# The first pair of K tiles: halved loads on two hardware queues, and copies divided over two engines

## The chip, the cores and the metric

The kernel runs on one core of one Trainium2 chip. The metric is the time of one execution on the device, in microseconds, as the median of several runs. The core has a matrix engine (TensorE, PE in the profile), a vector engine (VectorE, DVE), a scalar engine (ScalarE, ACT), a general engine (GpSimd, POOL) and a queue engine (SyncE, SP). Transfers are issued by SP, ACT and POOL, each into a queue of its own, and 16 DMA engines serve all of these queues.

## The reference

The inputs are float32: `a` and `b` are 2048 x 2048, `gamma` has 2048 elements, `eps` is 1e-5.

```python
x = np.matmul(a, b)
rms = np.sqrt(np.mean(x ** 2, axis=-1, keepdims=True) + eps)
return (gamma * x / rms).astype(np.float32)
```

Every row of the product is divided by its root mean square and multiplied by `gamma`.

## The kernel before, in words

Rows of `a` are handled in 16 blocks of 128. K is cut into 16 tiles of 128, which are taken in eight *pairs*. B has a left and a right half of 1024 columns, and each half has two chunks of 512. TensorE needs A with K on the partitions, so A is transposed first.

The work has three stages. In the *head*, row blocks 0 to 3 are multiplied by the left half of B while both arrive, pair by pair. Then the same four blocks meet the right half, and after that the other twelve blocks follow in groups of two, by seven products in place of eight (Strassen's scheme, with sums of quarters made on VectorE). In the last stage each block is scaled and stored.

The change touches the head alone, and in it pair 0. For pairs 1 to 7 of the head, POOL issues two loads each (`load_head`, L104): 128 columns by two of A for four row blocks into `early`, and the two tiles of B's left half into `raw` (L99). Both convert float32 to bfloat16 on the way. They are issued in the order of the pairs, pairs 1 to 3 at the start (L128, L131), pair 4 and later from within the loop over the pairs (L436). POOL's ninth and later loads each wait for the landing of the one issued eight before, since a completion semaphore is used again; this keeps eight loads in flight.

Pair 0 goes another way. Its part of A (`a0f`, 512 rows of 256 columns) is loaded as float32 by SP, and its two tiles of B (`b0f[0]` and `b0f[1]`, 128 x 1024 each) as float32 by ACT. Both lie in `early`. In `transpose_first` (L150) TensorE transposes A's eight 128 x 128 blocks, four of K tile 0 into one PSUM bank and four of K tile 1 into another. Each bank is moved to `head_at`, as bfloat16, in two moves of 128 x 256. Each tile of B is cast to bfloat16 in two halves of 512 columns, the first by VectorE and the second by ScalarE, into `raw[0][0]`. All four moves are on VectorE. Ahead of this, TensorE does eleven matmuls of zeros (L145), which nothing reads.

After it, `stream` (L397) does the pair's matmuls: seven (row block, chunk) groups for K tile 0, then the same seven for K tile 1. The order of the groups is (block 0, chunk 0), (block 0, chunk 1), (block 1, chunk 0) and so on, so the second matmul reads the second half of the cast tile. After twelve matmuls of pair 0 (seven in later pairs) TensorE transposes A of the next pair (`transpose_head`, L167), and VectorE copies that bank to `head_at` (L177). The eighth group, block 3 with chunk 1, has no accumulator of its own for the whole head; its two matmuls of a pair go to the bank that the transposes use (`stream_in_parts`, L411, L415), so they wait for VectorE's copy at L177.

The order on every engine is the order in which the program is written: the schedule is manual. Semaphores for the data are added by the framework.

Of the kernel before, what the change touches and what calls it, by code (L numbers as in the profile page):

```python
# [17 lines left out]
def kernel(  # L18
# [13 lines left out]
    nc = tc.nc  # L32
    P = 128
# [4 lines left out]
    W2 = 2 * P  # L38
    MB = M // P
    CH = 512  # L40
    NCH = N // CH
    HALF = N // 2
    HB = 4
# [16 lines left out]
    head_at = consts.tile([P, KT, HB, P], BF16, name="head_at")  # L60
    raw = [[consts.tile([P, 2, HALF], BF16, name=f"b_{j}_{kp}") for kp in range(KP)]
           for j in range(2)]
# [4 lines left out]
    a0f = early[:, 0:2048].bitcast(FP32).rearrange("p (r k) -> p r k", r=HB)  # L67
    b0f = [early[:, 2048 + t * 2048:2048 + (t + 1) * 2048].bitcast(FP32) for t in range(2)]
# [19 lines left out]
        return (at_even, at_odd)[(mb // 2) % 2][:, mb % 2]  # L88


    nc.sync.dma_start(out=a0f, in_=a[0:HB * P, 0:W2].rearrange("(r p) k -> p r k", p=P))
    for t in range(2):
        nc.scalar.dma_start(out=b0f[t], in_=b[t * P:(t + 1) * P, 0:HALF])

    def ah(kp):
        return ah_slot[(kp - 1) % NAH]
# [53 lines left out]
    def transpose_first():  # L150
        bank = [ps_t.tile([P, CH], FP32, name="tbank"), ps_a.tile([P, CH], FP32, name="acc")]
        view = [b.rearrange("p (r m) -> p r m", r=HB) for b in bank]
        for t in range(2):
            for r in range(HB):
                nc.tensor.matmul(view[t][:, r, :], a0f[:, r, t * P:(t + 1) * P], identity_f,
                                 is_transpose=True, start=(r == 0), stop=(r == HB - 1))
        for t in range(2):
            cast_first = [lambda: nc.vector.tensor_copy(out=raw[0][0][:, t, :CH],
                                                        in_=b0f[t][:, :CH]),
                          lambda: nc.scalar.copy(out=raw[0][0][:, t, CH:], in_=b0f[t][:, CH:])]  # L160
            move = [lambda h=h: nc.vector.tensor_copy(
                out=head_at[:, t, 2 * h:2 * h + 2, :], in_=view[t][:, 2 * h:2 * h + 2, :])
                for h in range(2)]
            for work in (cast_first + move if t == 0 else move + cast_first):
                work()

    def transpose_head(kp):  # L167
        bank = ps_t.tile([P, CH], FP32, name="tbank")
# [263 lines left out]
    for r in range(HB):  # L432
        x_tile(r, 0)
    early_sums = {4: ((2,), 0, 6), 5: ((5,), 0, 7), 6: ((1,), 0, KP)}
    transpose_first()
    for kp in range(KP):  # L436
        if kp + 4 < KP:
# [391 lines left out]
```

## Time and profile before

| What | us |
|---|---|
| median of 7 runs | 222.59 (222.46 to 222.88) |
| profiled execution | 222.4 |
| its span on the core | 220.6 |
| TensorE busy | 209.0 (95% of the span) |
| VectorE busy | 167.9 (76%) |
| ScalarE busy | 128.0 (58%) |
| GpSimd busy | 26.7 (12%) |

Times in the profile count from the start of the span. A line of a timeline gives the start, the time from the first instruction's start to the last one's end, the engine, the source line, the operation, the tile that it writes and the tiles that it reads, the shape, the number of instructions, and in brackets the idle time of the engine before them with what ended it. Matmuls overlap: one of 512 columns is shown for about 0.38 us while the next one starts 0.215 us after it. An entry in the chain of work gives start, length and what the time was spent on. The tile `early` stands for several things: under SP and ACT it is the float32 of pair 0, under POOL it is A of a later pair. The tile `b` is `raw`.

### The profile page before, as it was taken

The page shows a single profiled execution, that of the slowest core. Times are in us where ns is not written, and L with a number is a line of the kernel's source. Part 1 is how long each engine was busy: PE and PEld are TensorE (multiplying, and loading weights), DVE is VectorE, ACT ScalarE, POOL GpSimd, SP SyncE. Part 2 cuts the span into 40 slices and gives each one's busy share as a digit, 9 for nine tenths or more (in the row PEclk, how much of TensorE's full clock was granted, in tenths as well). Part 3 has the DMA queues.
Part 4 walks back from the last instruction along what each step waited for, and adds up shares of the span by engine and source line. Part 5 has one row for each costly group of instructions (what it writes and reads, how often), then busy time and mean ns, then how long its engine had stood idle before and what let it go on. Part 6 is the DMA issues. An engine that isn't in the chain of part 4 may idle for free.

```text
span 220.6 us, 2997 instructions
## 1 busy us (share of the span) xinstructions
PE 209.0 (95%) x1015; PEld 97.8 (44%) x1035; DVE 167.9 (76%) x330; ACT 128.0 (58%) x263; POOL 26.7 (12%) x56
## 2 busy tenths in 40 slices
PE   7999999999999999999999999999999999999950
PEld 2445444444455444444444444444444444444430
DVE  2428889999989898959697649855894769797691
ACT  3110002920798898479856997299738995334580
POOL 7624232210010002100010002000200000000000
PEclk9999999999999999999999999999999999999996
DMA  6999999999948695945799349945798449044045
GB/s 188 222 202 210 203 207 211 212 211 235 426 152 325 208 294 117 352 177 132 229 303 400 107 88 271 376 194 95 204 296 357 79 89 390 15 190 193 1 192 190
DMA packets 36465, 47.13 MB, mean 214 GB/s; under 512 B 21985, under 2 KB 26081, under 8 KB 35041
## 3 DMA queue, kind: packets, MB, share of 16 engines
q0 software_dynamic: 9936, 23.33, 41.8%
q1 hardware_dynamic: 26080, 22.29, 33.5%
q10 hardware_dynamic: 432, 1.31, 2.0%
q8 instruction: 8, 0.13, 0.2%
q14 instruction: 9, 0.07, 0.1%
HBM read 34.60 MB, written 16.78 MB: 233 GB/s over the span
## 4 chain that ended last, share of the span: by engine, by line
PE 83%; DMA 8%; POOL 3%; DVE 2%; issue 1%; ACT 1%; DVEq 0%; ACTq 0%; POOLq 0%
PE acc L289 69%; PE acc L384 12%; DMA b<-in_b_dram 8%; POOL early L105 1%; DVE x L709 1%; POOL b L99 1%; DVE x L712 1%; PE tbank L415 1%; PE tbank L172 1%; ACT sq L307 0%; PE tbank L189 0%; PE acc L189 0%; DVEq L824 0%; ACT sq L774 0%; DVE x L782 0%
## 5 line engine op out<-in xcount | busy, mean ns | idle before, releaser
L289 PE MATMUL acc<-b,s 128*128 128x512 bf16 x397 | 91.5, 379 | 0.6
L289 PEld LDWEIGHTS <-s 128*128 128x128 f16 (+1 forms) x512 | 49.9, 98 | 59.9 <-DVE s L264 0.4
L384 PE MATMUL acc<-b,head_at 128*128 128x512 bf16 x171 | 41.2, 379 | 0.6 <-DMA b<-in_b_dram 0.3
L307 ACT ACTIVATE sq<-x 128x512 bf16<-128x512 f32 x54 | 34.0, 630 | 6.9 <-DVE x L709 3.0
L366 DVE SCALAR_TENSOR_TENSOR x<-x,r,gamma_sb 128x1024 f32<-128x1024 f32 x28 | 34.8, 1281 | 0.7
L223 ACT ACTIVATE sq<-a 128x1024 bf16<-128x1024 f32 x24 | 25.3, 1054 | 3.3 <-DMA a<-in_a_dram 2.9
L384 PEld LDWEIGHTS <-head_at 128*128 128x128 bf16 x176 | 16.8, 98 | 19.8 <-issue 0.9
L246 ACT ACTIVATE head_at<-a,s 128x2048 f16<-128x2048 f32 x10 | 20.0, 1998 | 3.7 <-DVE s L233 3.7
L426 ACT COPY x<-acc 128x512 f32<-128x512 f32 x6 | 3.4, 588 | 25.0 <-PE acc L384 25.0
L289 PEld LDWEIGHTS <-head_at 128*128 128x128 f16 (+1 forms) x112 | 11.0, 98 | 13.3 <-issue 0.2
L289 PE MATMUL acc<-early,head_at 128*128 128x512 bf16 x63 | 14.4, 379 | 0.1
L289 PEld LDWEIGHTS <-at_even 128*128 128x128 f16 x96 | 9.4, 98 | 11.3
L289 PE MATMUL acc<-early,s 128*128 128x512 bf16 x55 | 14.2, 379 | 0.0
L264 DVE TENSOR_TENSOR s<-head_at 128x1024 f16<-128x1024 f16 (+5 forms) x22 | 13.4, 635 | 0.1
L596 DVE TENSOR_TENSOR x<-x,x 128x512 f32<-128x512 f32 x9 | 6.2, 693 | 8.8 <-ACT x L594 8.3
L99 POOL DMA_DIRECT2D b<-in_b_dram x15 | 10.6, 708 | 15.3 <-DMA b<-in_b_dram 12.7
L578 ACT COPY x<-acc 128x512 f32<-128x512 f32 x9 | 5.2, 574 | 11.5 <-PE acc L289 11.5
L289 PE MATMUL acc<-t_left,s 128*128 128x512 bf16 x47 | 11.3, 379 | 0.1
L280 DVE TENSOR_TENSOR b<-b 128x1024 bf16<-128x1024 bf16 x16 | 10.8, 685 | 0.2
L289 PE MATMUL acc<-early,at_even 128*128 128x512 bf16 x48 | 10.9, 379 | 0.1
L289 PE MATMUL acc<-t_left,head_at 128*128 128x512 bf16 x48 | 10.8, 379 | 0.0
L289 PE MATMUL acc<-t_left,at_even 128*128 128x512 bf16 x47 | 10.8, 379 | 0.1
(106 smaller groups left out, 214.9 us busy)
## 6 DMA issues: line engine op xcount, KB each, us to landing
out_dram<-x SPq DMA_DIRECT2D x30, 512.0 KB, 3.8
a<-in_a_dram POOLq DMA_DIRECT2D x10, 1024.0 KB, 8.6
b<-in_b_dram POOLq DMA_DIRECT2D x15, 512.0 KB, 16.8
a<-in_a_dram POOLq DMA_DIRECT2D x4, 512.0 KB, 16.7
early<-in_a_dram POOLq DMA_DIRECT2D x7, 256.0 KB, 14.7
early<-in_b_dram ACTq DMA_DIRECT2D x2, 512.0 KB, 5.8
gamma_sb<-in_gamma_dram POOLq DMA_DIRECT2D x1, 1024.0 KB, 14.8
out_dram<-x SPq DMA_DIRECT2D x3, 256.0 KB, 3.5
```

The costliest lines, as they stand in the source:

```text
L99: nc.gpsimd.dma_start(out=raw[j][kp], in_=b[kp * W2:(kp + 1) * W2, j * HALF:(j + 1) * HALF].rearrange("(t p) n -> p t n", p=P))
L223: nc.scalar.activation(out=junk, in_=a32[mb][:, h * HALF:(h + 1) * HALF], func=ACTF.Square, scale=2.0 ** -8, accum_out=n2[:, h:h + 1])
L246: nc.scalar.activation(out=a16[mb], in_=a32.pop(mb), func=ACTF.Copy, scale=factor.pop(mb))
L264: nc.vector.tensor_tensor(out=sum_of(g, s)[:, lo:hi, :], in0=x[:, lo:hi, :], in1=y[:, lo:hi, :], op=op)
L280: nc.vector.tensor_tensor(out=flat[:, 1:3, :], in0=flat[:, 1:3, :], in1=flat[:, 0::3, :], op=ALU.add)
L289: nc.tensor.matmul(bank, lhsT[:, kp, :], rhs, start=(start and kp == 0), stop=(kp == KP - 1), skip_group_check=not start)
L307: nc.scalar.activation(out=sq[:, 0:CH], in_=src, func=ACTF.Square, scale=inv_sqrt_n, accum_out=msq[mb][:, c:c + 1])
L366: nc.vector.scalar_tensor_tensor(out=x, in0=x, scalar=inverse_of[mb], in1=gamma_sb[:, h * HALF:(h + 1) * HALF], op0=ALU.mult, op1=ALU.mult)
L384: nc.tensor.matmul(bank, head_at[:, kt, r, :], head_rhs(c, kt), start=(kt == 0), stop=(kt == KT - 1))
L426: copy(out=x_chunk(*g), in_=banks[g])
L578: nc.scalar.copy(out=c, in_=one[1])
L596: nc.vector.tensor_tensor(out=t, in0=t, in1=x12, op=ALU.add)
```

## The change

Pair 0's part of A is loaded in two halves, row blocks 0 and 1 by SP and row blocks 2 and 3 by ACT. Each tile of B is loaded in two halves of 64 partitions, the lower by SP and the upper by ACT, after the half of A on the same queue. A row of B's load is 1024 float32, 4 KB, as before. So there are six transfers in place of three, of the same bytes.

The moves of K tile 0 stay on VectorE, and the moves of K tile 1 go to ScalarE. The casts change engines within tile 0: the first half of the columns is now cast by ScalarE and the second by VectorE; in tile 1 the first is VectorE's and the second ScalarE's, as before. The order on VectorE becomes: two moves of tile 0, cast of tile 0's second half, cast of tile 1's first half. On ScalarE it becomes: cast of tile 0's first half, two moves of tile 1, cast of tile 1's second half. Matmuls and their order are the same.

```diff
-    nc.sync.dma_start(out=a0f, in_=a[0:HB * P, 0:W2].rearrange("(r p) k -> p r k", p=P))
+    queues = (nc.sync, nc.scalar)
+    for h, queue in enumerate(queues):
+        queue.dma_start(out=a0f[:, 2 * h:2 * h + 2, :],
+                        in_=a[2 * h * P:(2 * h + 2) * P, 0:W2].rearrange("(r p) k -> p r k", p=P))
     for t in range(2):
-        nc.scalar.dma_start(out=b0f[t], in_=b[t * P:(t + 1) * P, 0:HALF])
+        for h, queue in enumerate(queues):
+            lo, hi = h * P // 2, (h + 1) * P // 2
+            queue.dma_start(out=b0f[t][lo:hi, :], in_=b[t * P + lo:t * P + hi, 0:HALF])
...
-        for t in range(2):
-            cast_first = [lambda: nc.vector.tensor_copy(out=raw[0][0][:, t, :CH],
-                                                        in_=b0f[t][:, :CH]),
-                          lambda: nc.scalar.copy(out=raw[0][0][:, t, CH:], in_=b0f[t][:, CH:])]
-            move = [lambda h=h: nc.vector.tensor_copy(
-                out=head_at[:, t, 2 * h:2 * h + 2, :], in_=view[t][:, 2 * h:2 * h + 2, :])
-                for h in range(2)]
-            for work in (cast_first + move if t == 0 else move + cast_first):
-                work()
+        copy = (nc.vector.tensor_copy, nc.scalar.copy)
+
+        def move(t):
+            for h in range(2):
+                copy[t](out=head_at[:, t, 2 * h:2 * h + 2, :], in_=view[t][:, 2 * h:2 * h + 2, :])
+
+        def cast(t, h):
+            copy[(t + h + 1) % 2](out=raw[0][0][:, t, h * CH:(h + 1) * CH], in_=b0f[t][:, h * CH:(h + 1) * CH])
+
+        cast(0, 0)
+        move(0)
+        cast(0, 1)
+        move(1)
+        cast(1, 0)
+        cast(1, 1)
```

## The prediction

> **What bounds the kernel now.** I read the chain that ended last first, then TensorE's timeline at the start, then the DMA rates there.
>
> The chain, in the page and in order of time:
>
> ```profile
> PE 83%; DMA 8%; POOL 3%; DVE 2%; issue 1%; ACT 1%; DVEq 0%; ACTq 0%; POOLq 0%
> ```
> ```profile
> 7.30 17.03 DMA b<-in_b_dram
> 24.34 0.04 issue
> 24.38 1.67 PE acc L384 x7
> ```
>
> To 24.34 us the chain is one transfer: the load of B's pair 4, issued by POOL at 7.30. From 24.38 to 207.5 it is TensorE alone, without a wait over 0.05 us. So the change can only act through what starts pair 4 at 24.38: that load, or TensorE being ready. How ready it was:
>
> ```profile
> 1.45 4.58 PE L145 MATMUL acc<-sq 128*128 128x512 bf16 x11 [1.45 <-DVE pace L135]
> 6.50 0.63 PE L155 MATMUL tbank<-t_left,early 128*128 128x128 f32 x4 [0.47 <-POOL msq L212]
> ...
> 7.64 2.76 PE L384 MATMUL acc<-b,head_at 128*128 128x512 bf16 x12
> ...
> 11.64 0.59 PE L415 MATMUL tbank<-b,head_at 128*128 128x512 bf16 x2 [0.35 <-DVE head_at L177]
> 12.23 1.46 PE L384 MATMUL acc<-b,head_at 128*128 128x512 bf16 x6
> ...
> 23.50 0.59 PE L415 MATMUL tbank<-b,head_at 128*128 128x512 bf16 x2
> 24.38 1.67 PE L384 MATMUL acc<-b,head_at 128*128 128x512 bf16 x7 [0.28 <-DMA b<-in_b_dram]
> ```
>
> A 512-column matmul is shown for 0.38 and the next starts 0.215 after it. The last of pair 3 starts at 23.50 + 0.59 - 0.38 = 23.71, so pair 4 could start at 23.93 and starts at 24.38: 0.45 is lost to the load. In the same way pair 1 could start at 12.07 and starts at 12.23; B's pair 1, issued at 2.13, lands 10.1 later, at 12.2. Pairs 1 to 3 take 11.70 (12.23 to 23.93) with no wait.
>
> The copies of the first pair on VectorE, and after them those on ScalarE:
>
> ```profile
> 5.11 0.76 DVE L158 CAST b<-early 128x512 bf16<-128x512 f32 x1 [1.28 <-DMA early<-in_b_dram]
> 7.17 0.75 DVE L161 CAST head_at<-tbank 128x256 bf16<-128x256 f32 x2 [1.30 <-PE tbank L155]
> 7.84 0.74 DVE L161 CAST head_at<-acc 128x256 bf16<-128x256 f32 x2
> 8.54 0.43 DVE L158 CAST b<-early 128x512 bf16<-128x512 f32 x1
> ```
> ```profile
> 5.10 0.62 ACT L160 CAST b<-early 128x512 bf16<-128x512 f32 x1 [1.92 <-DMA early<-in_b_dram]
> 8.53 0.62 ACT L160 CAST b<-early 128x512 bf16<-128x512 f32 x1 [2.81 <-DMA early<-in_b_dram]
> ```
>
> The DMA engines in 2 us windows (last columns: clock, DMA busy share, GB/s), and the queues' packets, MB and share from 6.0 to 7.5 us:
>
> ```profile
> 2.00:4.00 2.00, 2.00 (x7) 0.63 (x6) 0.36 (x2) 1.17 (x2) 1.93 (x5) 1.00 0.90 250
> 4.00:6.00 2.00, 2.00 (x6) 0.60 (x4) 0.76 (x1) 0.62 (x1) 2.00 (x4) 1.00 0.99 324
> 6.00:8.00 2.00, 1.45 (x11) 1.07 (x11) 0.83 (x3) 0.00 (x0) 2.00 (x11) 1.00 0.84 232
> 8.00:10.00 2.00, 2.00 (x11) 0.88 (x9) 0.96 (x3) 0.62 (x1) 0.07 (x2) 1.00 1.32 208
> ```
> ```profile
> q10 hardware_dynamic: 80, 0.33, 68.4%
> q0 software_dynamic: 40, 0.02, 9.8%
> ```
>
> POOL's queue (q0) has work from 2.1 us on, yet from 6.0 to 7.5 it moves 0.02 MB; only when the ACT queue (q10) has finished B's second tile, at 8.5 (issued 1.2, 7.3 to landing), does it run at its own 213 GB/s. Between, with one hardware queue left, the engines are busy 84% and move 232 GB/s, against 352 from 3.0 to 4.5 when SP's and ACT's both ran (the DMA view by windows: 0.17 MB in all from 1.5 to 3.0, 352 GB/s to 4.5, 313 to 6.0; SP's own 0.18 MB by 4.5; POOL's 0.13 MB from 7.5 to 8.5). From 8.5 on POOL's queue never runs dry (each issue waits for the landing of the one eight before). So what its stream gains or loses by 8.5 arrives, unchanged, at pair 4.
>
> **The change, part by part.**
>
> *Transposes (path).* They start at 6.50, once A has landed (issued 0.74, 5.6 later: 6.34). In halves on two queues A lands sooner: 0.17 MB had moved by 3.0, the other 0.35 MB at 352 GB/s take 1.0, and some 0.3 passes to the landing, so 4.3. At worst both queues ramp as slowly as SP's did (0.18 MB by 4.5), which gives 5.4. In either case TensorE is still in its warming matmuls: the last two run 0.76 from 5.27, so the last starts at 5.65 and the transposes can follow at 5.87, 0.63 sooner.
>
> *VectorE's new order (path).* Its first move starts 0.67 after the first transpose (7.17 - 6.50): 6.54. Moves follow each other by 0.34. Now both moves of tile 0, then the cast of B's second half, stand ahead of TensorE's second matmul; before, tile 0's casts were done by 5.87. The cast starts at 7.22 and takes 0.43 or 0.76 (both are in the rows; POOL was issuing during the long one, and is at this place again, 6.54 to 8.05). The second matmul so starts at 7.70 to 8.03. It now starts at 7.87 (the first two, 7.64 and 0.61 long, less 0.38). That eats nearly all of the 0.63: 0.17 won to 0.16 lost.
>
> *ScalarE (hidden).* It takes over two moves of 128x256 from PSUM. No row has this shape on ScalarE; between its 128x1 (0.20) and its 128x512 copy (0.59) I take 0.4 each. Tile 1's transposes end 1.06 after the first one starts, 6.93; moves to 7.75 (8.1 at 0.59), second cast 0.62, done by 8.4 (8.75). Tile 1's second matmul needs it seven matmuls after 7.70, at 9.2. Cover 0.45 to 0.8; beyond it TensorE waits one for one. VectorE's cast of tile 1 ends by 8.4.
>
> *DMA issues (hidden).* Six instead of three, 0.45 each. SP's queue has nothing else until its stores. On ACT the third pushes the table load from 1.69 to about 2.14; load 1.28 and root 0.20 end at 3.6, two us before the first cast. Two fewer VectorE moves and two more on ScalarE wait for nobody else.
>
> *TensorE to pair 4.* The wait of 0.35 at L415 (VectorE's copy of pair 1, after two matmuls) stays. Pair 1 can start at 12.07 less 0.17 or plus 0.16, 11.90 to 12.23, and pair 4 is ready 11.70 later: 23.60 to 23.93. TensorE's side so allows a gain of 0.45 to 0.78.
>
> *POOL's stream (path).* The three hardware loads are 1.57 MB. After 0.17 MB by 3.0, the rest, 1.40 MB, at the 352 GB/s of two queues takes 4.0: all read by 7.0, landed about 7.1; at the 313 GB/s of 4.5 to 6.0 it is 7.6. POOL's queue, if it gets nothing before, then needs 0.26 MB / 213 GB/s = 1.2 for A's pair 1 and 0.35 to its last engine: 8.7 to 9.2, where it now lands at 9.7 (1.24 + 8.5). Gain 0.5 to 1.0. Lower bound: the hardware loads still end at 8.5, and POOL's queue loses the 0.15 MB it moved before (0.02, and 0.13 to 8.5): 0.7 later. I take 0.8, inside the upper pair, since two queues are busy throughout and the 84% window is the place where time was lost.
>
> The Trainium skill, "DMA: Bandwidth & Descriptors", section "Rules for kernel authors", speaks against this: two transfers to disjoint partition halves serialize on the same 16 engines and one transfer of 128 partitions is better, and spreading loads over issuers does not help bandwidth. By it POOL's stream gains nothing, and the sum is 0. The rows differ from the rule in the 84% window alone, where one queue did not fill the engines; I go by the rows.
>
> *Sum.* Pair 4 of B lands at 24.34 - 0.8 = 23.5, TensorE is ready at 23.60 to 23.93: the later decides, a gain of 0.45 to 0.78, middle 0.6. Later pairs of B have 0.1 us of slack (pair 5 lands at 12.48 + 15.7 = 28.2 for a start at 28.27), but they move with the stream. After that TensorE's chain and the tail are unchanged. The profiled run took 222.4 (span 220.6 and 1.8 around it), 0.2 under the median of 222.59. So 222.4 - 0.6 = 221.8 there, 222.0 as a median.
>
> **Rivals.**
>
> 1. *The early transfers only change places.* POOL's stream keeps its times within 0.45, and pair 4 waits as now. For: every DMA engine serves all queues, and the bytes are the same. Against: 0.84 of busy share at 6 to 8. Time: 222.6 at no shift, 222.2 to 223.0 in all.
> 2. *Slower: POOL's queue starts later.* Two hardware queues hold the engines to 8.5 and the 0.02 + 0.13 MB are lost: pair 4 at 25.04, up 0.7: 223.3. For: POOL's queue got a twentieth of the bytes beside one hardware queue. Against: it needs halves that move no faster than one 128-partition load. It decides from a shift of 0.45 on.
> 3. *The first pair itself is late.* If B's first tile lands after 7.2, the cast on VectorE waits. At a landing of 8.1 the second matmul starts near 8.9 and pair 4 at 24.8, 0.4 late; at 8.5 it costs 0.5 to 0.8: 223.1 to 223.4. Against: 1.05 MB at 352 GB/s from 3.0 on land by 5.7.
>
> **How the numbers follow.** Forecast 0.50, rivals 0.30, 0.15 and 0.05. A measurement here tells about 0.2% (0.45 us) from no change. Faster is the forecast, 0.50. Same is the first rival and a part of the third, 0.31. Slower is the rest, 0.19. The forecast's own range is 221.8 to 222.2. For 8 in 10 I reach from 221.6 (a gain of 1.0, if the stream gives 1.0 and the copies are quicker than the rows) to 223.1, which takes in the first rival and leaves out the dearer half of the others.
>
> **What would show it.** Right: transposes near 5.9, second matmul of L384 between 7.7 and 8.0, POOL's first load landed by 9.2, pair 4 started by 23.93 with little or no wait for B. Wrong: the transposes behind a DMA still, or pair 4 again waiting for B after 24.3. It fails if POOL's queue does not start sooner, or if VectorE's cast runs past 8.03.

## The result, and the profile after

The changed kernel takes 225.97 us in the median of 12 runs (224.04 to 229.04), the kernel before 222.62 (30 runs, 222.30 to 223.07). The ratio is 1.0129, with a 95% interval from 1.0111 to 1.0147: slower by 1.3%, where 222.0 was forecast with a range to 223.1. The two highest runs, 228.35 and 229.04, count as slow ones and stand outside the ratio. The profiled execution took 226.38 (span 224.6), 3.98 more than the one before.

The chain that ended last, in order of time, no longer begins with POOL's load of pair 4. It begins with a half of a tile of pair 0:

```profile
1.27 8.34 DMA early<-in_b_dram
9.63 0.63 ACT b L169
10.30 4.07 PE acc L395 x12
14.38 0.81 PE tbank L183 x8
```

TensorE's timeline (start, length, operation, idle time ahead with its releaser) has nearly the whole loss:

```profile
5.45 0.60 PE L160 MATMUL tbank<-t_left,early 128*128 128x128 f32 x4
5.88 0.60 PE L160 MATMUL acc<-t_left,early 128*128 128x128 f32 x4
10.30 4.07 PE L395 MATMUL acc<-b,head_at 128*128 128x512 bf16 x12 [3.82 <-ACT b L169]
14.17 1.01 PE L183 MATMUL tbank<-identity,early 128*128 128x128 bf16 x8
...
16.39 1.46 PE L395 MATMUL acc<-b,head_at 128*128 128x512 bf16 x6
...
28.09 1.68 PE L395 MATMUL acc<-b,head_at 128*128 128x512 bf16 x7
```

The transposes start earlier than before (5.45 against 6.50), and then TensorE idles 3.82 us for ScalarE's cast. Pair 1 (16.39) starts 4.16 later than before, pair 4 (28.09) 3.71 later: 0.45 is given back where before waited for B's pair 4. Behind that the difference is carried on: where the chain passes from TensorE to VectorE near the end it is 3.66 (211.14 against 207.48), and the span is 3.94 longer.

The two casting engines, VectorE and then ScalarE, show that they wait for a transfer and not for each other:

```profile
6.09 0.76 DVE L166 CAST head_at<-tbank 128x256 bf16<-128x256 f32 x2 [2.26 <-PE tbank L160]
9.63 0.43 DVE L169 CAST b<-early 128x512 bf16<-128x512 f32 x1 [2.79 <-DMA early<-in_b_dram]
```
```profile
9.63 0.62 ACT L169 CAST b<-early 128x512 bf16<-128x512 f32 x1 [5.39 <-DMA early<-in_b_dram]
10.16 0.64 ACT L166 CAST head_at<-acc 128x256 bf16<-128x256 f32 x2
```

A transfer has landed when the last of its 16 engines has reported. The landings, read from the trace for each transfer: A's halves 3.83 and 4.53; tile 0 of B 5.89 (lower half, SP) and 9.61 (upper half, ACT); tile 1 10.25 and 11.35; then A's pair 1 from POOL at 10.61. The upper half of tile 0 has arrived from eight of the 16 engines by 7.18, from fifteen by 8.48, and the cast waits for the sixteenth.

What the queues moved from 1.5 to 8.5 us (q0 is POOL's, q1 SP's, q10 ACT's: packets, MB, share of the engines), before and then after:

```profile
q10 hardware_dynamic: 288, 1.05, 52.6%
q1 hardware_dynamic: 528, 0.52, 22.1%
q0 software_dynamic: 296, 0.15, 15.8%
```
```profile
q1 hardware_dynamic: 420, 0.77, 40.0%
q10 hardware_dynamic: 384, 0.66, 33.6%
q0 software_dynamic: 465, 0.25, 28.8%
```

The sums are 1.72 and 1.68 MB, and from 1.5 to 10.0 they are 2.04 and 2.03. (POOL's bytes are counted as bfloat16: a load of two tiles of B is 512 KB.) With two hardware queues the engines moved more from 2 to 4 us (330 GB/s against 250) and less from 4 to 6 (221 against 324), and no more in all. POOL's queue got 0.10 MB more by 8.5, and the hardware loads, which pair 0 needs first, 0.14 MB less.

There is a second loss. The windows around it (busy us of PE, PEld, DVE, ACT, POOL; then clock, DMA share, GB/s):

```profile
10.00:11.57 1.57, 1.27 (x6) 0.58 (x6) 0.26 (x2) 0.99 (x4) 0.68 (x1) 1.00 1.12 208
11.57:14.98 3.41, 3.41 (x15) 1.72 (x14) 0.32 (x1) 0.42 (x1) 1.56 (x3) 0.50 1.27 210
14.98:20.00 5.02, 4.62 (x29) 2.33 (x28) 1.38 (x2) 0.58 (x1) 1.47 (x2) 1.00 1.24 201
```

For 3.41 us TensorE is granted half its clock; the twelve matmuls of pair 0 take 4.07 in place of 2.76.

### The profile page after: what moved, and what is told of

It is laid out like the page before. It is cut to its first block, busy times and chain, and to the rows that moved or that the text cites. A ratio compares the mean times of both kernels' runs of the same rounds, so it can differ in the third digit from the quotient of the medians.

```text
span 224.6 us, 3009 instructions
## 1 busy us (share of the span) xinstructions
PE 209.6 (93%) x1015; PEld 98.5 (44%) x1035; DVE 166.8 (74%) x328; ACT 128.5 (57%) x265; POOL 26.7 (12%) x56
## 3 DMA queue, kind: packets, MB, share of 16 engines
q10 hardware_dynamic: 576, 1.05, 1.6%
## 4 chain that ended last, share of the span: by engine, by line
PE 89%; DMA 4%; DVE 3%; ACT 1%; issue 1%; DVEq 0%; ACTq 0%
PE acc L300 67%; PE acc L395 17%; DMA early<-in_b_dram 4%; PE tbank L183 2%; PE tbank L426 2%; DVE x L720 1%; DVE x L723 1%; ACT sq L318 0%; PE tbank L200 0%; PE acc L200 0%; DVE head_at L188 0%; DVEq L835 0%; ACT b L169 0%; ACT sq L785 0%; ACTq L93 0%
## 5 line engine op out<-in xcount | busy, mean ns | idle before, releaser
L395 PE MATMUL acc<-b,head_at 128*128 128x512 bf16 x171 | 42.5, 389 | 4.0 <-ACT b L169 3.8
```

The source lines that it names most:

```text
L395: nc.tensor.matmul(bank, head_at[:, kt, r, :], head_rhs(c, kt), start=(kt == 0), stop=(kt == KT - 1))
```

## The experiments

Theories at the outset. *Loads*: the halved transfers are at fault, because tile 0 lands late. *Copies*: the new order of moves and casts is at fault, because second halves now stand behind moves. Within the first: *order* (both queues carry A ahead of B, where ACT carried B first), *halves* (a tile in two transfers is slower than in one) and *POOL* (its queue gets in between). And *clock*: part of the loss follows from TensorE's idle time.

### Copies alone, and loads alone

The copies of the changed kernel behind the three loads of the one before:

```diff
     nc.sync.dma_start(out=a0f, in_=a[0:HB * P, 0:W2].rearrange("(r p) k -> p r k", p=P))
     for t in range(2):
         nc.scalar.dma_start(out=b0f[t], in_=b[t * P:(t + 1) * P, 0:HALF])
...
-            for work in (cast_first + move if t == 0 else move + cast_first):
-                work()
+        cast(0, 0)
+        move(0)
+        cast(0, 1)
+        move(1)
+        cast(1, 0)
+        cast(1, 1)
```

> The copies as changed, the three loads as before. Copies theory (VectorE's and ScalarE's new order is what is slow): 225 us or more. Order theory (A ahead of B on both queues lets POOL's queue in before B has landed) and halves theory (transfers of 64 partitions are slow by themselves): the copies alone cost little. The transposes stay at 6.5, so the moves stay at 7.17 and VectorE's cast of tile 0 runs 7.85 to 8.3 or 8.6; TensorE's second matmul is 0.4 to 0.8 late, of which the 0.45 lost before pair 4 takes up most: 222.4 to 223.0 us. TensorE has no idle time over 1 us at the start and its clock stays at 1.00.

Measured: 222.44 against 222.63, ratio 0.9996 (0.9986 to 1.0006). TensorE's timeline:

```profile
7.54 0.39 PE L390 MATMUL acc<-b,head_at 128*128 128x512 bf16 x1
8.36 2.53 PE L390 MATMUL acc<-b,head_at 128*128 128x512 bf16 x11 [0.42 <-DVE b L164]
...
24.59 1.67 PE L390 MATMUL acc<-b,head_at 128*128 128x512 bf16 x7 [0.18 <-DMA b<-in_b_dram]
```

The second matmul does wait 0.42 for VectorE's cast, and starts at 8.36 in place of 7.87. But pair 4 still ends in a wait for B: the slack of 0.45 there takes the lateness up. The copies are not the cause.

The six loads with the old copies:

```diff
     for t in range(2):
         for h, queue in enumerate(queues):
             lo, hi = h * P // 2, (h + 1) * P // 2
             queue.dma_start(out=b0f[t][lo:hi, :], in_=b[t * P + lo:t * P + hi, 0:HALF])
...
-        cast(0, 0)
-        move(0)
-        cast(0, 1)
-        move(1)
-        cast(1, 0)
-        cast(1, 1)
+            for work in (cast_first + move if t == 0 else move + cast_first):
+                work()
```

> The six loads as changed, the copies as before. Copies theory: 222.6 us or less. Order and halves theories: about the changed kernel, 225 to 227 us, B's first tile landing at 8 to 10 us, and in most runs a stretch of 3.4 us at half the clock; some tenths more than the changed kernel, since VectorE's moves now stand behind a cast that waits for B.

Measured: 226.29 (224.04 to 227.10, 4 runs), ratio 1.0149 (1.0094 to 1.0204): as slow as the whole change. In its profiled execution (224.04, the fastest of the four, in which the clock held) tile 0 lands at 5.96 and 8.31, tile 1 at 10.06 and 10.62. The loads are the cause.

### Which part of the loads: order

A's halves on both queues, as in the change, but behind them whole tiles of B, one on each queue:

```diff
     for h, queue in enumerate(queues):
         queue.dma_start(out=a0f[:, 2 * h:2 * h + 2, :],
                         in_=a[2 * h * P:(2 * h + 2) * P, 0:W2].rearrange("(r p) k -> p r k", p=P))
-    for t in range(2):
-        for h, queue in enumerate(queues):
-            lo, hi = h * P // 2, (h + 1) * P // 2
-            queue.dma_start(out=b0f[t][lo:hi, :], in_=b[t * P + lo:t * P + hi, 0:HALF])
+    for t, queue in enumerate(queues):
+        queue.dma_start(out=b0f[t], in_=b[t * P:(t + 1) * P, 0:HALF])
```

> As the changed kernel, but each tile of B is one transfer of 128 partitions: tile 0 on SP behind its half of A, tile 1 on ACT behind the other half. Halves theory: tile 0 lands by 6 us, and the time is 222.6 us or less. Order theory: both tiles still come after A, beside POOL's queue; tile 0 lands after 7 us and the time is 224 to 226 us.

Measured: 222.85 (10 runs), ratio 1.0017 (0.9997 to 1.0037). With halved A and the new copies kept, whole tiles alone take away nearly all of the loss. TensorE:

```profile
9.04 2.75 PE L393 MATMUL acc<-b,head_at 128*128 128x512 bf16 x12 [1.85 <-ACT b L167]
...
25.15 1.67 PE L393 MATMUL acc<-b,head_at 128*128 128x512 bf16 x7
```

Order does have a price: tile 0 lands at 8.35, and the pair starts 1.4 late against 7.64. But tile 1 is there at 8.58, so nothing waits again, and half of the lateness is gone by pair 4 (25.15 against 24.38). The profiled execution took 223.29; the median lies below it.

If order were the main cause, tile 0 first would mend it:

```diff
+    load_tile(0)
     for h, queue in enumerate(queues):
         queue.dma_start(out=a0f[:, 2 * h:2 * h + 2, :],
                         in_=a[2 * h * P:(2 * h + 2) * P, 0:W2].rearrange("(r p) k -> p r k", p=P))
-    for t in range(2):
-        load_tile(t)
+    load_tile(1)
```

Here `load_tile` issues the two partition halves as the change does.

> As the changed kernel, in another order on both queues: the halves of tile 0 of B, then the halves of A, then the halves of tile 1. Order theory: tile 0 lands by 5 us, A by 6.4, tile 1 between 8 and 10, and the time is 222.0 to 223.0 us with the clock at 1.00 throughout the head. Halves theory: tile 0 lands after 7 us as in the changed kernel, 224 us or more.

Measured: 229.41, ratio 1.0302 (1.0279 to 1.0324), the slowest of all. Tile 0 lands at 4.28 and 5.32, and now the second half of A (issued at 1.36) lands at 11.99 and tile 1 at 11.43 and 13.29. What stands second on ACT is late, be it a half of A or, as in the change, of B; on SP the first half of A, second there, lands at 7.08. TensorE waits 4.41 in the middle of the transposes, and the clock is half from 10.44 to 17.27.

The third order tried keeps every tile whole and sends tile 0 ahead of A's second half on ACT, and tile 1 behind A's first half on SP (new copies, halved A):

```diff
+    load_tile(0, nc.scalar)
+    load_a(0, nc.sync)
+    load_a(1, nc.scalar)
+    load_tile(1, nc.sync)
```

> Whole tiles of B and A by halves: tile 0 of B and then the second half of A on ACT, the first half of A and then tile 1 of B on SP; copies as changed. If being among the first transfer of each queue is what keeps a load fast: tile 0 lands by 5.2 us, the half of A behind it at 6 to 7, tile 1 by 8.6, and the time is 222.2 to 222.9 us. If a split of A harms as the split of B did: the second half of A lands after 8 us and the time is 224 us or more.

Measured: 225.94, ratio 1.0138 (1.0110 to 1.0166). The tiles land early (5.14 and 8.49), but A's halves only at 6.28 and 8.78, so the transposes are split around a wait of 2.00, and the clock is half from 8.10 to 14.93, which is a part of this loss. So this order does not mend the kernel either; A in two halves was early only in the orders that send both halves first (3.89 and 4.19 with whole tiles behind).

### Which part of the loads: halves

The kernel before, with one edit: each tile of B in two halves of 64 partitions, all four on ACT.

```diff
     for t in range(2):
-        nc.scalar.dma_start(out=b0f[t], in_=b[t * P:(t + 1) * P, 0:HALF])
+        for h in range(2):
+            lo, hi = h * P // 2, (h + 1) * P // 2
+            nc.scalar.dma_start(out=b0f[t][lo:hi, :], in_=b[t * P + lo:t * P + hi, 0:HALF])
```

> The kernel before with one thing changed: each tile of B is loaded in two halves of 64 partitions, one behind the other, both on ACT; A whole on SP, copies as before. If 64 partitions are slow by themselves: a 4 KB packet takes near 290 ns instead of 180 to 205, tile 0 lands after 6 us (5.1 before), tile 1 after 9.5 (8.5 before), and the time is 223 us or more. If they are slow only behind A or on two queues at once: tile 0 by 5.4, tile 1 by 8.8, 222.4 to 222.9 us.

Measured: 224.91, ratio 1.0110 (1.0081 to 1.0138). No second hardware queue, no halved A, no new copies, and the loss is there: on this chip the changed kernel takes 224.53 (below). TensorE waits for each tile in turn; then the queues from 1.5 to 8.5 us:

```profile
8.69 1.68 PE L386 MATMUL acc<-b,head_at 128*128 128x512 bf16 x7 [1.65 <-DVE head_at L163]
12.16 1.24 PE L386 MATMUL acc<-b,head_at 128*128 128x512 bf16 x5 [1.78 <-DVE b L160]
```
```profile
q10 hardware_dynamic: 238, 0.79, 42.8%
q0 software_dynamic: 450, 0.26, 28.1%
q1 hardware_dynamic: 528, 0.52, 23.6%
```

POOL's queue has 0.26 MB by 8.5 as in the changed kernel, and the hardware loads 1.31 in place of 1.57. Tile 1 lands at 11.59 (after: 11.35). A's pair 1 lands at 11.74, 2.0 later than before, so POOL's stream does not win by what it takes early. The packets of 4 KB were expected to slow to some 290 ns; in the whole of both tiles they take 236 ns on average, where the kernel before has 228.

Is it the 64 partitions, or the two transfers? The same, cut by columns, 128 partitions and rows of 2 KB:

```diff
-            lo, hi = h * P // 2, (h + 1) * P // 2
-            nc.scalar.dma_start(out=b0f[t][lo:hi, :], in_=b[t * P + lo:t * P + hi, 0:HALF])
+            lo, hi = h * CH, (h + 1) * CH
+            nc.scalar.dma_start(out=b0f[t][:, lo:hi], in_=b[t * P:(t + 1) * P, lo:hi])
```

> The kernel before with each tile of B loaded in two halves of 512 columns (128 partitions of 2 KB each), one behind the other on ACT; all else as before. If it is the 64 partitions that cost the 2.3 us of the run with halved partitions on ACT alone: tile 0 lands by 5.5 us, tile 1 by 9, and the time is 222.4 to 223.0 us. If it is that there are two transfers where there was one: tile 0 at 6 to 8 us, tile 1 after 10, and 224 us or more.

Measured: 224.73, ratio 1.0091 (1.0074 to 1.0108). As slow as the partition halves, so the loss does not need transfers of 64 partitions: two transfers per tile in place of one are enough. Tile 0 lands at 5.09 and 7.63, tile 1 at 10.23 and 11.28, and TensorE waits twice within K tile 1:

```profile
10.73 0.38 PE L386 MATMUL acc<-b,head_at 128*128 128x512 bf16 x1 [0.95 <-DVE b L160]
11.97 1.07 PE L386 MATMUL acc<-b,head_at 128*128 128x512 bf16 x4 [0.86 <-ACT b L162]
```

From 1.5 to 8.5 POOL's queue moves 0.16 MB, hardly more than before, and the hardware queues 1.38. That sum hides two things. From 2 to 4 us, with POOL's queue still empty, the engines move only 135 GB/s (250 before); this was seen in one execution, and its cause is open. And from 6 to 8 us POOL's queue gets in here too, the kernel before first:

```profile
q10 hardware_dynamic: 111, 0.41, 64.2%
q0 software_dynamic: 107, 0.05, 19.9%
```
```profile
q10 hardware_dynamic: 170, 0.32, 64.8%
q0 software_dynamic: 217, 0.11, 48.4%
```

The changed kernel with its tile halves by columns, one on each queue:

```diff
-            lo, hi = h * P // 2, (h + 1) * P // 2
-            queue.dma_start(out=b0f[t][lo:hi, :], in_=b[t * P + lo:t * P + hi, 0:HALF])
+            lo, hi = h * CH, (h + 1) * CH
+            queue.dma_start(out=b0f[t][:, lo:hi], in_=b[t * P:(t + 1) * P, lo:hi])
```

> As the changed kernel, but each tile of B is halved by columns (128 partitions of 2 KB) and not by partitions (64 of 4 KB). If 64 partitions are what is slow: the tiles land by 8.6 us, as the whole tiles behind A did, and the time is 222.4 to 223.3 us. If it is that there are four smaller transfers behind A beside POOL's queue: the tiles land at 9.5 to 11.5 us as in the changed kernel, 225 to 227 us.

Measured: 224.14, ratio 1.0078 (1.0053 to 1.0104), less slow than the changed kernel in its first runs (1.0129), but not clear of its runs on another chip (1.0093, below). Tile 0 now lands at 6.34 and 6.80, but tile 1 at 10.38 and 10.69 as there, and TensorE waits for it after seven matmuls:

```profile
7.90 1.46 PE L395 MATMUL acc<-b,head_at 128*128 128x512 bf16 x6 [0.27 <-DVE b L169]
10.88 1.52 PE L395 MATMUL acc<-b,head_at 128*128 128x512 bf16 x5 [1.53 <-DVE b L169]
```

### POOL's share

The changed kernel, with POOL's first load held until tile 1 has landed (a small copy on POOL that reads the tile). POOL's whole stream is late by this, so its total time tells nothing; the landings up to 9 us do.

```diff
-    load_head(1)
     identity_f = t_left[:, 2, KP - 1, 0:2 * P].bitcast(FP32)
     make_identity(nc, identity_f)
+    landed = consts.tile([P, 1], FP32, name="landed")
+    nc.gpsimd.tensor_copy(out=landed, in_=b0f[1][:, 0:1])
+    load_head(1)
```

> As the changed kernel, but POOL issues its first load only after both tiles of B have landed (it copies a column of the second tile first). Sharing theory (the halved loads are slow because POOL's queue moves its 1 KB rows beside them): without it the six transfers run at 310 to 350 GB/s, tile 0 lands by 6.0 us and tile 1 by 7.5. Theory that halved transfers are slow by themselves: the upper half of tile 0 still lands after 8 us. The time says little, since POOL's stream starts some 6 us later: about 225 us or more.

Measured (one execution, 231.6): tile 0 at 5.80 and 6.92 in place of 5.89 and 9.61, tile 1 at 8.77 and 8.94 in place of 10.25 and 11.35. Neither theory's numbers came: it is between them. By these figures 2.7 us of tile 0's lateness, and 2.4 of tile 1's, come from POOL's queue working beside the loads. Four more profiles of the same six loads (tile 0 by 8.31 to 9.48, tile 1 by 10.45 to 10.88) give 1.4 to 2.6 and 1.5 to 1.9. What is left is not POOL's: with the engines to themselves the halves land no sooner (8.94) than whole tiles that share them with POOL (8.51 before, 8.58 behind halved A). Whole tiles with POOL's queue held back were not run. From 4 to 6 us POOL's queue moves next to nothing in this kernel and in the one with whole tiles behind halved A, so that stretch compares the two kinds, halves first:

```profile
DMA packets 141, 0.45 MB, mean 225 GB/s; under 512 B 31, under 2 KB 31, under 8 KB 141
```
```profile
DMA packets 142, 0.57 MB, mean 287 GB/s; under 512 B 0, under 2 KB 2, under 8 KB 142
```

A fifth fewer bytes. Of the halves' packets 31 carry next to nothing; the other 110, and 140 of the whole tiles', have some 4 KB each. The engines are as busy in both: the two hardware queues take 60.6 + 41.7% of them with the halves, 55.2 + 48.4% with the whole tiles. Over 2 us of 16 engines that makes about 0.30 us for a packet of the halves and 0.24 for one of the whole tiles. And in the changed kernel that same stretch is already POOL's for half of the engines' time:

```profile
q0 software_dynamic: 225, 0.12, 48.8%
q10 hardware_dynamic: 57, 0.21, 45.7%
q1 hardware_dynamic: 44, 0.11, 20.5%
```

### The clock

Sixteen matmuls of zeros, which nothing reads, behind the transposes of the changed kernel, so that TensorE does not idle:

```diff
+        for _ in range(16):
+            nc.tensor.matmul(warm_bank, warm[:, 0:P], warm[:, 0:CH], start=True, stop=True)
         copy = (nc.vector.tensor_copy, nc.scalar.copy)
```

> As the changed kernel, but TensorE does 16 more matmuls of zeros, which nothing reads, between the transposes and the first matmul of pair 0 (3.4 us at full clock, in the 3.8 us of idle time). Clock theory (about 1.5 us of the loss is the stretch of 3.4 us at half clock after the idle time): clock 1.00 through the head, 224.0 to 224.8 us, and a smaller spread between runs. Rival (the whole loss is B's late landing): as the changed kernel, 225.5 to 226.5 us.

Measured: 225.06 (224.83 to 226.29, 4 runs), ratio 1.0121 (1.0090 to 1.0153), profiled 224.84. The clock stays at 1.00 through the head and the pair takes 2.75, but the median is not clearly under that of the changed kernel. So both were run side by side on one chip, the changed kernel with no edit, and the filled one again:

> The changed kernel once more, on the same chip as the next one. Clock theory: runs with the stretch of half clock 225.6 to 227 us at a mean clock of 0.97 to 0.98, runs without it 224.0 to 224.5 at 0.99; median 225.5 to 226.4.

> The changed kernel with 16 more matmuls of zeros, which nothing reads, between the transposes and pair 0, on the same chip as the one before it. Clock theory: every run at a mean clock of 0.987 or more, 224.5 to 225.3 us, 0.7 to 1.2 us below the changed kernel, with intervals that do not touch. Rival (the half clock costs nothing in the end): the same time as the changed kernel.

Measured: 224.53 (223.79 to 226.05, 6 runs) without fill, ratio 1.0093 (1.0056 to 1.0130); 224.73 (224.34 to 225.53, 6 runs) with it, ratio 1.0091 (1.0071 to 1.0111). No difference: the gain that was expected of the fill is missed, and so is the median expected without it. Two things in the profiles bear on it. The first is that the zeros themselves can hold up pair 0. ScalarE, then TensorE, with the second fill:

```profile
8.80 0.62 ACT L171 CAST b<-early 128x512 bf16<-128x512 f32 x1 [4.55 <-DMA early<-in_b_dram]
```
```profile
7.17 3.62 PE L163 MATMUL acc<-sq 128*128 128x512 bf16 x16
10.63 2.75 PE L397 MATMUL acc<-b,head_at 128*128 128x512 bf16 x12
```

Without fill the pair's first matmul starts 0.67 after ScalarE's cast begins (10.30 and 9.63). Here the cast begins at 8.80 and the matmul at 10.63, behind the zeros, 1.16 later than that; in the first filled profile (9.46 and 10.47) it is 0.34. The second is that the changed kernel does not always lose the clock. In its second profile, TensorE and then the window:

```profile
10.17 2.75 PE L395 MATMUL acc<-b,head_at 128*128 128x512 bf16 x12 [3.66 <-ACT b L169]
...
14.58 1.46 PE L395 MATMUL acc<-b,head_at 128*128 128x512 bf16 x6
```
```profile
11.57:14.98 3.41, 3.06 (x21) 1.52 (x19) 0.69 (x1) 0.20 (x1) 1.51 (x3) 1.00 1.24 208
```

It idles as long (3.66 against 3.82), tile 0 is as late (9.48), but the clock does not fall. The execution took 224.56 against 226.38: 1.82 less, which is the 1.81 by which pair 1 starts sooner (14.58 against 16.39): 0.13 because pair 0 starts sooner (10.17 against 10.30), 1.68 for the clock. So the same program may or may not pay for the clock. The ten runs behind the first ratio fit this. Three lie at 224.04 to 224.31 with a mean clock of 0.987 to 0.993, seven at 225.65 to 226.57 with 0.979 to 0.982; 3.41 us at half speed take 3.41 x 0.5 / 222 = 0.008 off the mean. That the seven have such a stretch was seen in one profile and is otherwise inferred. On the second chip four of six runs are at 224.56 or below. The other two, 226.05 and 225.97, have a mean clock of 0.986, where 0.97 to 0.98 was expected; the kernel before has 0.987 to 0.993 there, so these two are not shown to have such a stretch. What decides between the two is not settled.

## Why the prediction was wrong

Of the loss of 3.98 in the profiled run, pair 0's late B is 2.48 and the clock 1.68, and 0.45 is given back at pair 4: 3.71 there. (In the execution whose clock held, pair 1 starts at 14.58 in place of 12.23, 2.35 late, with pair 0 begun 0.13 sooner.) The remaining 0.27 arises behind TensorE's work, at the end of the run, and is not explained.

- *Transposes, gain 0.63.* Right in kind: A landed at 3.83 and 4.53 (4.3 forecast), the transposes came at 5.45, 1.05 sooner. The 0.42 beyond the forecast came from the warming matmuls, which ended at 5.61 in place of 6.03 without being changed. It bought nothing, as TensorE then had no B.
- *VectorE's new order, second matmul at 7.70 to 8.03.* Its working took tile 0 to be there; the casts waited for it to 9.63. The order's own cost was measured apart, in the copies alone: the second matmul starts 1.96 after the first transpose (8.36 and 6.40), where the working had 1.83 to 2.16, and the whole takes 222.44. That term was right.
- *ScalarE's moves, hidden.* Right in size (0.64 for both, where 0.8 was taken). They run at 10.16 behind a cast that waits for B, a queueing that the step had not named.
- *DMA issues, hidden.* Right: ScalarE's table load begins at 2.75 (2.14 forecast) and ends at 4.03, over five us before the cast.
- *TensorE ready for pair 4 at 23.60 to 23.93.* Wrong by 4.2 to 4.5 (28.09), through the late B and the clock.
- *POOL's stream, gain 0.8.* This is the step that failed. It took the remaining 1.40 MB of hardware loads at 352 GB/s, all landed by 7.1 to 7.6, with POOL's queue getting nothing meanwhile. They landed by 11.35. By the same rate A and tile 0 were to land by 5.7, early enough for pair 0; tile 0 landed at 9.61. The rate of 352 was that of whole transfers of a 512 KB A and a 512 KB tile; partition halves of tiles moved at 225 GB/s from 4 to 6 us even with POOL's queue held back. And POOL's queue, with 0.02 MB from 6.0 to 7.5 before, had 0.12 MB from 4 to 6 and as much from 6 to 8. A queue that had stood back beside a whole-tile load was taken to stand back beside half-tile loads too; no row showed that. Even beside the whole tile it did not stand back to the end: it is said to run only from 8.5, but by the forecast's own figures it moved 0.13 MB from 7.5 to 8.5, with that tile still in flight. The gain of the stream itself was 0.45 (0.30 in the second profile) and was worth nothing.
- *Where the forecast weighed row against rule.* The 84% window was taken as room that a second queue would fill. From 1.5 to 10.0 us the bytes are equal, 2.04 and 2.03 MB, and partition halves alone cost 1.1%. The Trainium skill, "DMA: Bandwidth & Descriptors", section "Rules for kernel authors", advises one 128-partition transfer over two to partition halves and expects no bandwidth from more issuers. Both fit what was measured over the whole of the loads. Its reason, that the halves serialize, would make the sum 0; the loss of 1.1% goes beyond it.
- *Rivals.* The first (nothing moves) and the second (POOL later) both fall: POOL's load of pair 4 lands at 23.89, 0.45 sooner than before, just within what the first allowed, but TensorE no longer waits for it. The third, that tile 0 lands after 7.2, is what happened. Its chance of 0.05 rested on 352 GB/s once more, and its price stopped at a landing of 8.5. By its working pair 4 starts 16.7 after the landing (8.1 to 24.8); for the execution with a steady clock, where tile 0 landed at 9.48, that gives 26.2, and 26.28 was measured, 1.90 late. The clock was in no case of the forecast.

What stays open: why a tile in two transfers loses the engines to POOL's queue. The bytes of each queue show that it does, in partition halves (0.25 and 0.26 MB by 8.5 us against 0.15) and from 6 to 8 us in column halves (0.11 against 0.05). Open too is why a 4 KB packet of partition halves took 0.30 us from 4 to 6 us where one of whole tiles took 0.24. How an engine chooses between its queues cannot be seen in these records. No version beat the kernel before: its head had 0.45 us to win at pair 4, and the copies alone, with 0.9996, did not win it.

## What to carry to other kernels

Do not cost a split transfer at the rate of the whole one: look at what the last part to land releases, and at which other queues have work waiting, since a queue that stands back beside one large load need not beside several small ones. If the first tiles gate the kernel, each in one transfer was best here. An earlier start of a first step is worth nothing until the next operand is there as well.

## What was not expected of the hardware

- Halving two transfers of 512 KB, with nothing else edited, cost 2.3 us (222.60 to 224.91 on one chip), whether by partitions or by columns (2.2, 222.57 to 224.73).
- The engines finish a transfer unevenly beside POOL's queue: tile 0's upper half came from eight engines by 7.18 and from the last at 9.61; without POOL by 6.53 and 6.92.
- TensorE's granted clock halved for 3.41 us after an idle stretch of 3.82, and not after one of 3.66 in the same program. In the kernel with column halves alone it halved from 12.82 to 16.23 though no wait for B ahead of it was longer than 0.95. In both traces the changes of the clock lie 3.41 or twice that apart (4.74, 11.57, 14.98 and 5.99, 12.82, 16.23), so the step of 3.41 just ahead of the half clock is the one to look at. TensorE is busy for 1.27 of it in the changed kernel and for 1.60 with column halves, where several short waits add up. In the profile whose clock held, 1.46 is busy in the step from 8.21 to 11.63, counted from a change at 4.80. So no limit comes out of these figures. The Trainium skill, "TensorE: Matmul & The Clock Gate", Part 1, puts the throttled state down to an idle window of about 3.4 us. The length of the stretch agrees; in neither case was TensorE idle throughout the step ahead.
